# A two-layer diffusion backbone on one core: the opening of the second ConvFFN, the places of the last adaLN gate's additions, two product sums' places in the first ConvFFN, and copies ahead of casts on ScalarE

## The chip, the core and the metric

The kernel runs on one core of one Trainium2 chip. The time is device microseconds of one launch; the figure of a kernel is the median of its runs. A profile is one further execution, with its own time. Five engines work in parallel, each through its own list of instructions in order: PE (matrix products), DVE and ACT (elementwise work), POOL, and SP, which here issues most transfers from HBM. An instruction that must wait holds up everything behind it in its engine's list.

## The reference

512 latent tokens of width 1024 pass two layers. Layer 0 mixes tokens by attention, layer 1 by a Fourier transform. Every layer ends with a gated ConvFFN, which is where this change lies:

```python
def conv_ffn(h, w_up, conv_w, conv_b, w_down):
    u = h @ w_up                                   # 1024 -> 2 x 2816
    up = jnp.pad(u, ((0, 0), (1, 1), (0, 0)))
    u = up[:, :-2] * conv_w[0] + up[:, 1:-1] * conv_w[1] + up[:, 2:] * conv_w[2] + conv_b
    gate, val = jnp.split(u, 2, axis=-1)
    return (jax.nn.silu(gate) * val) @ w_down      # 2816 -> 1024
...
        sh1, sc1, g1, sh2, sc2, g2 = adaln_params(c, mod_w[i], mod_b[i])   # silu(c) @ mod_w[i] + mod_b[i], in six
...
        h = modulate(rms_norm(x, norm_g[i, 2]), sh2, sc2)
        x = x + g2 * rms_norm(conv_ffn(h, ffn_w_up[i], ffn_conv_w[i], ffn_conv_b[i], ffn_w_down[i]), norm_g[i, 3])
```

Each of the six adaLN vectors of a layer is a vector times a 1024x1024 matrix. The kernel calls the matrix `mod_r`, and computes most of these products in the shadow of other work.

## The kernel before

**Precision.** Every float32 product is made of three reduced-precision matmuls of 128x128 weights against 256 tokens (lines 108, 109 and 110): high part times high part, low times high, high times low. A weight tile is loaded raw from HBM; ACT casts it to the high part `wh`, and DVE subtracts to get the low part `wl` (both on line 144). The activations of a stage lie ready in pairs: `hh` and `hl` are the FFN's input, `xh` and `xl` (or `xT`) the gated results.

**ConvFFN.** The 2816 inner channels are 22 units of 128 channels, numbered 0 to 21; each has a gate half and a value half (two up products of 1024 by 128), a convolution (one ACT instruction on line 1485, two DVE instructions on lines 1486 and 1488 for each half), a silu, a product and a split into high and low. Units are collected in groups (`GROUPS`); a finished group is multiplied by its part of `w_down` in eight down tiles of 128 output channels. In FFN 1 (layer 1) the down tiles are spread among the units of the next group by the table `DOWN`: so many after unit so and so. What a down tile gives is added to `yT` by DVE (line 1511).

**Seven-product units.** Units in the table `SEVEN` compute both halves with seven products of half size instead of eight (a Strassen-like scheme). `seven_weights` loads the unit's two weight blocks, forms sums of them on DVE (lines 1389, 1391 and 1392) and then splits four pieces: "1", "57", "63" and "24", in that order. `seven_products` issues the products in the order "1", "5", "6", "2", "3", "4", "7" into two PSUM tiles `x` and `y`. Between them ACT copies halves of these tiles away (lines 1422, 1424 and 1426), since the next product but one overwrites or adds to them. After "3", DVE adds `xs` to `x` (line 1429); after "7" it adds `ys` to `y` (line 1433). "5" and "7" need the weights "57"; "6" and "3" need "63"; "2" and "4" need "24".

**The adaLN products** come in two forms. In FFN 0, `gemv_jobs` runs several of them one after the other, a step at a time, whenever the FFN calls `pump(gem, ...)`: each step is two DVE additions of a 128x1024 tile (line 594 or 597) and the next load of `mod_r`. At the end of one product `gemv_end` issues its "sums": four matmuls (line 639) that add up over partitions, an ACT copy, and later two transposes (line 649) and the vector's own small arithmetic on DVE. In FFN 1 `gemv_pair` does the last vector, the gate `g2` of layer 1: four pairs of additions (lines 627 and 629), each pair on two tiles `xh` and `xl` of 512 KB that one SP transfer each brings. These steps are pumped after the down tiles that `GEMV` names, group by group.

**Opening of FFN 1.** Units 0 to 2 begin while the normalisation before them is still being finished. `NSKEW[1]` is 5, so that five half-units are begun in the sweep; the sixth entry of `first` is unit 2's value half, and unit 3 (`FIRST`) is the first ordinary one. In the program `halves` are tokens 0 to 255 and 256 to 511, `hl` of the second half becomes ready piece by piece.

**What sets the order.** Nothing is written down as a fixed list: a scheduler orders each engine's instructions from the program's order, its dependences, `follow(a, b)` (a directly behind b), `behind_pe` (behind the PE work issued so far) and `held`. So a moved call can move other engines' rows too.

Of the kernel before, what the change touches and what calls it, by code (L numbers as in the profile page):

```python
# [2 lines left out]

# [7 lines left out]
F32 = mybir.dt.float32  # L11
# [4 lines left out]
ALU = mybir.AluOpType  # L16
# [3 lines left out]
P = 128  # L20
D = 1024
KC = D // P
T = 512
TT = T // P
HT = T // 2
# [7 lines left out]
FIRST = 3  # L33

SUMS = [5, 7]
# [1 line left out]
SEVEN = [(5, 6, 8, 10, 12, 14, 15, 17, 18, 20), (8, 9, 10, 11, 12, 13, 14, 15, 16, 17, 18, 19, 20, 21)]  # L37


GEMV = {0: (0, 5, 7), 1: (0, 2, 4, 6)}  # L40
DOWN = {8: 4, 9: 4, 10: 1, 11: 1, 12: 1, 13: 2, 14: 1, 15: 2, 16: 1, 17: 1, 18: 1, 19: 2, 20: 1, 21: 2}
NSKEW = [6, 5]
EPS = 1e-6
# [42 lines left out]
def kernel(ctx: ExitStack, tc: tile.TileContext, a):  # L86
    nc = tc.nc
# [55 lines left out]
    def split(h, l, src, eng=V):  # L143
        i = S.copy(out=h, in_=src), eng.tensor_tensor(out=l, in0=src, in1=f(h), op=ALU.subtract)  # L144
        for j in i:
            held(j)
        return i
# [414 lines left out]
    def gemv_jobs(jobs, pps, away=None):  # L562
        places = away and [xT[:, 4 * i:4 * i + 4, :].rearrange("p a b -> p (a b)").rearrange(
            "p (i d) -> p i d", i=2) for i in range(2)]
        todo = [(l, v, kk) for l, v in jobs for kk in range(4)]
        ws = []

        def load():
            if len(ws) < len(todo):
                l, v, kk = todo[len(ws)]  # L570
                src = a["mod_r"][6 * l + v - 2, kk]
                if not places:
                    ws.append(raw([P, 2, D], src))
                    return
                ws.append(places[len(ws) % 2])
                SY.dma_start(out=ws[-1], in_=src)

        if places:
            SY.dma_start(out=away, in_=xT)
            for _ in places:  # L580
                load()
            yield
        n = 0
        for l, v in jobs:
            acc = mk(cp, [P, D], F32, "gacc", 1)
            for kk in range(4):
                if not places:
                    load()
                w = ws[n]
                n += 1  # L590
                for i in range(2):
                    k = 2 * kk + i
                    if k == 0:
                        held(V.tensor_scalar(out=acc, in0=w[:, i, :], scalar1=scol[:, 0, k:k + 1], scalar2=None,
                                             op0=ALU.mult))
                    else:
                        held(V.scalar_tensor_tensor(out=acc, in0=w[:, i, :], scalar=scol[:, 0, k:k + 1], in1=acc,  # L597
                                                    op0=ALU.mult, op1=ALU.add))
                if places:
                    load()  # L600
                yield
            if places and (l, v) == jobs[-1]:
                SY.dma_start(out=xT, in_=away)
            end = gemv_end(l, v, acc, pps)
            next(end)
            yield
            if (l, v) == jobs[-1]:
                yield
            next(end, None)
# [3 lines left out]
    def gemv_pair(l, v, pps, xp):  # L613
        w = [mk(xp.first, [P, D], F32, n, 4) for n in ("xh", "xl")]

        def load(kk):
            for i in range(2):
                SY.dma_start(out=w[i], in_=a["mod_r"][6 * l + v - 2, kk][:, i, :])

        load(0)  # L620
        yield
        acc = mk(cp, [P, D], F32, "gacc", 1)
        for kk in range(4):
            for i in range(2):
                k = 2 * kk + i
                if k == 0:
                    V.tensor_scalar(out=acc, in0=w[i], scalar1=scol[:, 0, k:k + 1], scalar2=None, op0=ALU.mult)
                else:
                    V.scalar_tensor_tensor(out=acc, in0=w[i], scalar=scol[:, 0, k:k + 1], in1=acc, op0=ALU.mult,
                                           op1=ALU.add)  # L630
            if kk < 3:
                load(kk + 1)
            yield
        yield from gemv_end(l, v, acc, pps)
# [701 lines left out]
    def up_weights(l, pairs, fis, eng=V):  # L1336
        for fi in fis:
            r = raw([P, 2, KC, P], a["w_up"][l, fi])
            for i in range(2):
                wh, wl = pairs([P, KC, P])  # L1340
                split(wh, wl, r[:, i, :, :], eng)
                yield [(wh[:, k, :], wl[:, k, :]) for k in range(KC)]
# [27 lines left out]
    def seven_inputs(xp):  # L1370
# [10 lines left out]
            split(*b[n], src)  # L1381
        return b

    def seven_weights(l, fi):
        r = raw([P, 2, KC, P], a["w_up"][l, fi])
        s = mk(wp, [P, 4, KH, P], F32, "raw", 3)
        a4 = r.rearrange("p i (c k) n -> p (i c) k n", c=2)

        for j in (V.tensor_tensor(out=s[:, 0:2], in0=a4[:, 3::-3], in1=a4[:, 2].unsqueeze(1).to_broadcast(
                      [P, 2, KH, P]), op=ALU.add),  # L1390
                  V.tensor_tensor(out=s[:, 2], in0=s[:, 0], in1=a4[:, 0], op=ALU.add),
                  V.tensor_tensor(out=s[:, 3], in0=s[:, 2], in1=a4[:, 1], op=ALU.add)):
            held(j)
        w = {}
        for names, src in (("1", a4[:, 0:1]), ("57", s[:, 0:2]), ("63", s[:, 2:4]), ("24", a4[:, 1::2])):
            wh, wl = wpair([P, len(names), KH, P])
            split(wh, wl, src)
            for i, n in enumerate(names):
                w[n] = wh[:, i], wl[:, i]
        return w  # L1400


    def seven_products(l, fi, pps, bs):
        w = seven_weights(l, fi)
        x, y = (mk(pps, [P, T], F32, "mm", 6) for _ in range(2))
        xs, ys = (mk(cp, [P, T], F32, "sq", 2) for _ in range(2))
        begun, last = {}, []

        def product(n, ps, h):
            (wh, wl), (bh, bl) = w[n], bs[n]  # L1410
            new = id(ps) not in begun
            m = []
            for k in range(KH):
                m += mm3(ps[:, halves[h]], wh[:, k, :], wl[:, k, :], bh[:, k, :], bl[:, k, :], new and k == 0,
                         k == KH - 1, True)
            begun[id(ps)] = True
            if last:
                follow(m[0], last.pop())
            last.append(m[-1])

        product("1", y, 1)
        S.copy(out=xs[:, :HT], in_=y[:, HT:])  # L1422
        product("5", x, 1)
        S.copy(out=ys[:, HT:], in_=x[:, HT:])  # L1424
        product("6", y, 1)
        S.copy(out=xs[:, HT:], in_=y[:, HT:])
        product("2", x, 0)
        product("3", x, 1)
        V.tensor_tensor(out=x, in0=x, in1=xs, op=ALU.add)  # L1429
        product("4", y, 0)  # L1430
        product("7", y, 1)
        S.copy(out=ys[:, :HT], in_=y[:, HT:])
        V.tensor_tensor(out=y, in0=y, in1=ys, op=ALU.add)
        return x, y
# [27 lines left out]
    def ffn(l, xp, ready, pre, mid, gem, plain=None):  # L1462
# [5 lines left out]
        def up_mm(ps, w, sl, k0=0):  # L1468
            return [mm3(ps[:, sl], wh, wl, bh[:, sl], bl[:, sl], k == 0, k == KC - 1)
                    for k, ((wh, wl), (bh, bl)) in enumerate(zip(w, H)) if k >= k0]  # L1470
# [155 lines left out]
        cg = None  # L1626
        for u, (fi, i, w, ps) in enumerate(first):
            if u == skew:
                for s in halves:
                    up_mm(ps, w, s)  # L1630
            elif plain is None and u > 1:
                up_mm(ps, w, halves[1], 1)
            c = conv(fi, i, ps, (R, *(ub[:, n, i, fi:fi + 1] for n in (3, 1, 2))) if u < skew and plain else None)
            if i == 0:
                cg = c
            else:
                gated(fi, cg, c, 0)
# [5 lines left out]
        for gi, (f0, nch) in enumerate(GROUPS[l]):  # L1643
            end = gi == len(GROUPS[l]) - 1
            for fi in range(max(f0, FIRST), f0 + nch):
                if fi == SUMS[l]:
                    bs = seven_inputs(xp)
                if fi in SEVEN[l]:
                    cc = [conv(fi, i, u, None, i == 1) for i, u in enumerate(seven_products(l, fi, pps, bs))]
                else:  # L1650
                    cc = []
                    for i, w in enumerate(up_weights(l, wpair, [fi])):
                        ps = mk(pps, [P, T], F32, "mm", 6)
                        m = [up_mm(ps, w, s) for s in halves]
                        follow(m[1][0][0], m[0][-1][1])
                        cc.append(conv(fi, i, ps))
                gated(fi, cc[0], cc[1], f0)
                if l == 0 and fi not in SEVEN[l] and fi > FIRST + 4:
                    pump(gem, GP[0])
                if l:  # L1660
                    pump(down, DOWN.get(fi, 0))
# [88 lines left out]
    with ExitStack() as es:  # L1750
# [177 lines left out]
        xp = Pairs(ctx)  # L1928
# [180 lines left out]
```

## Time and profile before

| | |
|---|---|
| median of 3 runs | 1092.1 us (1091.9, 1092.1, 1093.35) |
| profiled execution, its own time | 1095.22 us |
| its span (what the trace covers) | 1093.5 us |
| PE, DVE, ACT busy | 1074.4, 887.3, 601.7 us |
| granted TensorE clock, mean | 0.999 |

Times in the trace count from the start of the span. FFN 0 runs from about 320 to 642 us, the Fourier mixer lies between, FFN 1 runs from about 745 to 1082 us, and a tail of 11 us ends the program. A row of the timeline gives start and duration in us, the engine, the line, the operation, output and inputs, a count, and in brackets how long the engine was idle before and what ended that. Matmul durations overlap: a 128x256 matmul shows about 0.28 us, but the next starts 0.11 to 0.12 us later, so a pause on PE is read from starts. DVE's rows overlap too, by 0.08 us.

### The profile page before, as it was taken

Reading aid. Unit: us, or ns where it says so; the run is one execution under the profiler, and the core shown is the slowest. Engines: PE = TensorE matmul, PEld = TensorE weight load, DVE = VectorE, ACT = ScalarE, POOL = GpSimd, SP = SyncE. Lnnn points to the kernel's source line nnn. Section 1 sums busy time; section 2 is a strip of 40 time slices with the busy share of each in tenths; the row PEclk is TensorE's granted clock in tenths of the full one; section 3 lists DMA queues with packets and bytes.
Section 4 is the critical chain, followed back from the end, with each engine's and each line's share of the span. In section 5 each row is a group of like instructions: output and inputs, shape, how many; then the busy total and the mean of one; then the engine's idle time right before and its main releaser. Section 6 shows DMA issues by size and latency. Waiting matters only on the chain.

```text
span 1093.5 us, 22646 instructions
## 1 busy us (share of the span) xinstructions
PE 1074.4 (98%) x9432; PEld 1012.8 (93%) x9432; DVE 887.3 (81%) x1454; ACT 601.7 (55%) x1053; POOL 104.6 (10%) x114
## 2 busy tenths in 40 slices
PE   9999999999999999999999999999999999999997
PEld 5699888869999999999999999989999999999996
DVE  5778877774679976877999877878997899889855
ACT  4442365675656633552465566767755465556533
POOL 0046122522100000000000020100000000000012
PEclk9999999999999999999999999999999999999999
DMA  9776101174231473426724620743205533323342
GB/s 364 287 260 212 40 1 40 43 271 188 78 155 40 154 251 143 186 88 229 263 83 153 229 107 2 237 149 120 99 26 162 205 106 112 117 82 108 111 150 78
DMA packets 33912, 156.55 MB, mean 143 GB/s; under 512 B 3472, under 2 KB 8208, under 8 KB 22160
## 3 DMA queue, kind: packets, MB, share of 16 engines
q1 hardware_dynamic: 32656, 150.89, 38.0%
q0 software_dynamic: 1152, 4.19, 1.6%
q8 instruction: 74, 1.21, 0.4%
q14 instruction: 30, 0.25, 0.1%
HBM read 148.78 MB, written 6.29 MB: 142 GB/s over the span
## 4 chain that ended last, share of the span: by engine, by line
PE 81%; DVE 9%; DMA 4%; ACT 3%; issue 2%; SPq 0%; POOL 0%; DVEq 0%; ACTq 0%; POOLq 0%
PE mm L108 23%; PE mm L109 22%; PE mm L110 22%; DVE wl L144 2%; PE PT L1147 1%; DMA raw<-in_w_up 1%; DVE gacc L597 1%; DMA xT<-in_xT 1%; PE gm L108 1%; PE O L109 1%; PE gm L109 1%; PE gm L110 1%; PE misc L211 1%; PE O L108 1%; PE O L110 1%
## 5 line engine op out<-in xcount | busy, mean ns | idle before, releaser
L144 ACT CAST wh<-raw 128x1024 fp32r<-128x1024 f32 (+2 forms) x206 | 190.2, 931 | 153.1 <-PE mm L109 101.6
L144 DVE TENSOR_TENSOR wl<-raw,wh 128x1024 fp32r<-128x1024 f32 (+2 forms) x206 | 220.1, 1074 | 25.6 <-ACT wh L144 25.4
L108 PE MATMUL mm<-hh,wh 128*128 128x256 f32 x852 | 237.7, 280 | 2.2 <-ACT sq L1424 1.1
L109 PE MATMUL mm<-hl,wh 128*128 128x256 f32 x852 | 236.9, 278 | 0.3 <-DVE hl L393 0.3
L110 PE MATMUL mm<-hh,wl 128*128 128x256 f32 x852 | 236.4, 278 | 0.7 <-DVE wl L144 0.7
L108 PEld LDWEIGHTS mm<-hh,wh 128*128 128x128 f32 x852 | 159.7, 188 | 4.5 <-ACT sq L1424 1.5
L110 PEld LDWEIGHTS mm<-hh,wl 128*128 128x128 f32 x852 | 160.8, 189 | 1.5 <-DVE wl L144 1.4
L109 PEld LDWEIGHTS mm<-hl,wh 128*128 128x128 f32 x852 | 160.0, 188 | 0.7 <-DVE hl L393 0.5
L108 PE MATMUL mm<-xh,wh 128*128 128x256 f32 x492 | 136.8, 279 | 0.0
L109 PE MATMUL mm<-xl,wh 128*128 128x256 f32 x492 | 136.5, 278 | 0.0
L110 PE MATMUL mm<-xh,wl 128*128 128x256 f32 x492 | 136.1, 277 | 0.0
L108 PE MATMUL mm<-zh,wh 128*128 128x256 f32 x384 | 106.8, 278 | 0.1
L109 PE MATMUL mm<-zl,wh 128*128 128x256 f32 x384 | 106.3, 277 | 0.0
L110 PE MATMUL mm<-zh,wl 128*128 128x256 f32 x384 | 106.3, 277 | 0.0
L108 PEld LDWEIGHTS mm<-xh,wh 128*128 128x128 f32 x492 | 92.4, 188 | 1.3 <-issue 0.4
L109 PEld LDWEIGHTS mm<-xl,wh 128*128 128x128 f32 x492 | 92.4, 188 | 0.5 <-issue 0.4
L110 PEld LDWEIGHTS mm<-xh,wl 128*128 128x128 f32 x492 | 92.4, 188 | 0.0
L318 POOL TENSOR_TENSOR cv<-cv,sq 128x256 f32<-128x256 f32 x20 | 16.6, 830 | 711.8 <-ACT sq L316 711.1
L108 PEld LDWEIGHTS mm<-zh,wh 128*128 128x128 f32 x384 | 72.1, 188 | 0.8 <-ACT sq L1422 0.3
L110 PEld LDWEIGHTS mm<-zh,wl 128*128 128x128 f32 x384 | 72.3, 188 | 0.0
L109 PEld LDWEIGHTS mm<-zl,wh 128*128 128x128 f32 x384 | 72.1, 188 | 0.0
L1485 ACT ACTIVATE cv<-mm,cols 128x512 f32<-128x512 f32 x59 | 45.7, 776 | 13.7 <-DVE mm L1429 6.5
(469 smaller groups left out, 2784.1 us busy)
## 6 DMA issues: line engine op xcount, KB each, us to landing
raw<-in_w_up SPq DMA_DIRECT2D x42, 1024.0 KB, 4.8
xT<-in_mod_r SPq DMA_DIRECT2D x20, 1024.0 KB, 5.0
raw<-in_w_down SPq DMA_DIRECT2D x32, 384.0 KB, 3.1
raw<-in_mod_p SPq DMA_DIRECT2D x8, 1024.0 KB, 4.8
raw<-in_w_down SPq DMA_DIRECT2D x16, 512.0 KB, 4.7
raw<-in_w_in SPq DMA_DIRECT2D x6, 1024.0 KB, 8.3
yT<-in_mod_r SPq DMA_DIRECT2D x10, 512.0 KB, 5.8
raw<-in_w_out SPq DMA_DIRECT2D x4, 1024.0 KB, 5.9
```

The costliest lines, as they stand in the source:

```text
L108: i = PE.matmul(out, lhsT=ah, rhs=bh, start=start, stop=False, skip_group_check=skip)
L109: PE.matmul(out, lhsT=ah, rhs=bl, start=False, stop=False, skip_group_check=skip)
L110: return i, PE.matmul(out, lhsT=al, rhs=bh, start=False, stop=stop, skip_group_check=skip)
L144: i = S.copy(out=h, in_=src), eng.tensor_tensor(out=l, in0=src, in1=f(h), op=ALU.subtract)
L211: PE.matmul(ps[32 * j:32 * j + 32, :w], lhsT=ones32, rhs=sq[:, j * w:(j + 1) * w], start=first, stop=last)
L318: G.tensor_tensor(out=self.acc[:, sl], in0=self.acc[:, sl], in1=sq[:, sl], op=ALU.add)
L597: held(V.scalar_tensor_tensor(out=acc, in0=w[:, i, :], scalar=scol[:, 0, k:k + 1], in1=acc, op0=ALU.mult, op1=ALU.add))
L1147: PE.transpose(out=pt[:, j * P:(j + 1) * P], in_=Ps[j][:, off:off + P], identity=ident)
L1485: S.activation(out=cv, in_=ps, func=AF.Identity, bias=bc, scale=wc[1])
```

## The change

Five things, in the order of the program:

1. In FFN 0's `gemv_jobs`, for the third and the fourth product (jobs 2 and 3, `GAP = 2`): the third's sums are issued one pump later, its successor's first step runs without a pause behind that, and the fourth's sums are put behind the PE work issued so far.
2. In FFN 1 the sixth entry of the opening and unit 3's gate half (`FIRST`) are issued by halves of tokens: first half of the one, first half of the other, then the second halves.
3. `seven_inputs` of FFN 1 is called after unit 7 instead of before it.
4. `gemv_pair`'s additions are pumped at other places (`GEMV`), and each is given a dependence without a semaphore on the DVE instruction issued just before its pair, so that the scheduler can't move it ahead of that.
5. The copy after "6" of one seven-product unit is followed by the next unit's first cast on ACT.

```diff
-GEMV = {0: (0, 5, 7), 1: (0, 2, 4, 6)}
+GEMV = {0: (0, 7), 1: (1, 3, 5), 2: (0, 2)}
+GAP = 2
...
-                yield
+                if not (places and job == GAP + 1 and kk == 0):
+                    yield
...
             end = gemv_end(l, v, acc, pps)
-            next(end)
+            if places and job == GAP:
+                yield
+            if places and job == GAP + 1:
+                behind_pe(end)
+            else:
+                next(end)
...
         for kk in range(4):
+            last = [o for o in nc.cur_bb.bb.instructions if o.engine == mybir.EngineType.DVE][-1].name
             for i in range(2):
...
+                tc.add_manual_dep(j.ins, last, mybir.DependencyInfo(
+                    mybir.DependencyClass.NoSync, mybir.DependencyReason.DATA), reason="order")
...
-            split(wh, wl, src)
+            c = split(wh, wl, src)[0]
+            if names == "1" and copied:
+                follow(c, copied.pop())
...
-        S.copy(out=xs[:, HT:], in_=y[:, HT:])
+        copied.append(S.copy(out=xs[:, HT:], in_=y[:, HT:]))
...
             if u == skew:
-                for s in halves:
-                    up_mm(ps, w, s)
+                m = [up_mm(ps, w, halves[0])]
+                ahead = up_weights(l, wpair, [FIRST])
+                wa = next(ahead)
+                pa = mk(pps, [P, T], F32, "mm", 6)
+                m += [up_mm(pa, wa, halves[0]), up_mm(ps, w, halves[1])]
+                for j in (1, 2):
+                    follow(m[j][0][0], m[j - 1][-1][1])
...
-                if fi == SUMS[l]:
+                if fi == SUMS[l] and fi in SEVEN[l]:
                     bs = seven_inputs(xp)
...
+                    if fi == SUMS[l]:
+                        bs = seven_inputs(xp)
```

In the changed program the lines above carry other numbers: 108 to 110 become 110 to 112, 144 becomes 146, 1389, 1391 and 1392 become 1402, 1404 and 1405, 1422, 1424 and 1426 become 1437, 1439 and 1441, 1429 and 1433 become 1444 and 1448, 627 and 629 become 636 and 638, 1485, 1486 and 1488 become 1500, 1501 and 1503, 1511 becomes 1526. No engine's count of instructions changes. The rows below give a place in an engine's list, the line, the operation, output and inputs; the numbers behind a tile's name tell its copies apart.

**First place: PE at the opening of FFN 1.** `mm_9394` is the sixth entry of the opening. Before, after 24 matmuls on its first half of tokens:

```order
L110 MATMUL mm_9394<-hh_69,wl_9086 128x256
L108 MATMUL mm_9394<-hh_69,wh_9085 128x256
L109 MATMUL mm_9394<-hl_71,wh_9085 128x256
L110 MATMUL mm_9394<-hh_69,wl_9086 128x256
L108 MATMUL mm_9394<-hh_69,wh_9085 128x256
```

and now, with `mm_9478` the gate half of unit 3:

```order
L112 MATMUL mm_9394<-hh_69,wl_9086 128x256
L110 MATMUL mm_9478<-hh_69,wh_9474 128x256
L111 MATMUL mm_9478<-hl_71,wh_9474 128x256
L112 MATMUL mm_9478<-hh_69,wl_9475 128x256
L110 MATMUL mm_9478<-hh_69,wh_9474 128x256
```

Between the two halves of the sixth entry stand now 24 matmuls of unit 3 on the first half.

**Second place: ACT between units 11 and 12 of FFN 1.** The three copies of unit 11 are those into `sq`; the cast of 128x512 is the first of unit 12. Before:

```order
L1422 COPY sq_10681<-mm_10680 128x256
L144 CAST wh_10839<-raw_10833 128x512
L1424 COPY sq_10682<-mm_10679 128x256
L1426 COPY sq_10681<-mm_10680 128x256
L144 CAST wh_10843<-raw_10835 128x1024
```

and now:

```order
L1437 COPY sq_10677<-mm_10676 128x256
L1439 COPY sq_10678<-mm_10675 128x256
L1441 COPY sq_10677<-mm_10676 128x256
L146 CAST wh_10831<-raw_10825 128x512
L146 CAST wh_10835<-raw_10827 128x1024
```

The cast, which waits for a load, stood ahead of two copies that only wait for PE; now it stands behind them.

**Third place: DVE at unit 15 of FFN 1.** `mm_11423` (before) and `mm_11415` (now) are unit 14's tile `x`; the raw tile is that of unit 15's weight sums. The beginning of the block before:

```order
L1389 TENSOR_TENSOR raw_11577<-raw_11575 128x1024
L1511 TENSOR_TENSOR yT_68<-yT_68,mm_11357 128x512
L144 TENSOR_TENSOR wl_11534<-raw_11531,wh_11533 128x768
L1391 TENSOR_TENSOR raw_11577<-raw_11577,raw_11575 128x512
L144 TENSOR_TENSOR wl_11582<-raw_11575,wh_11581 128x512
L1392 TENSOR_TENSOR raw_11577<-raw_11577,raw_11575 128x512
L1429 TENSOR_TENSOR mm_11423<-mm_11423,sq_11425 128x512
```

and now, all of its rows that the prediction counts (in two pieces):

```order
L1444 TENSOR_TENSOR mm_11415<-mm_11415,sq_11417 128x512
L1402 TENSOR_TENSOR raw_11571<-raw_11569 128x1024
L146 TENSOR_TENSOR wl_11576<-raw_11569,wh_11575 128x512
L1501 SCALAR_TENSOR_TENSOR cv_1416_11509<-mm_11415,cols_64,cv_1416_11509 128x511
L1404 TENSOR_TENSOR raw_11571<-raw_11571,raw_11569 128x512
L1448 TENSOR_TENSOR mm_11416<-mm_11416,sq_11418 128x512
L1503 SCALAR_TENSOR_TENSOR cv_1416_11509<-mm_11415,cols_64,cv_1416_11509 128x511
L1405 TENSOR_TENSOR raw_11571<-raw_11571,raw_11569 128x512
```

```order
L1501 SCALAR_TENSOR_TENSOR cv_1417_11513<-mm_11416,ncw_9535,cv_1417_11513 128x511
L146 TENSOR_TENSOR wl_11580<-raw_11571,wh_11579 128x1024
L1503 SCALAR_TENSOR_TENSOR cv_1417_11513<-mm_11416,ncw_9535,cv_1417_11513 128x511
L1526 TENSOR_TENSOR yT_68<-yT_68,mm_11529 128x512
L1514 TENSOR_TENSOR cv_1417_11513<-cv_1416_11509,cv_1417_11513 128x512
L638 SCALAR_TENSOR_TENSOR gacc_10648<-xh_10292,cols_64,gacc_10648 128x1024
L146 TENSOR_TENSOR wl_11584<-raw_11571,wh_11583 128x1024
L638 SCALAR_TENSOR_TENSOR gacc_10648<-xl_10293,cols_64,gacc_10648 128x1024
L146 TENSOR_TENSOR wl_11588<-raw_11569,wh_11587 128x1024
```

Unit 14's addition into `x` stands now ahead of unit 15's weight sums, and the fourth pair of the gate's additions stands ahead of and behind the low part of "63" (`wl_11584`), ahead of that of "24" (`wl_11588`). On PE the four sums of the gate, which stood ahead of unit 14's product "1", now stand behind the second matmul of unit 15's "2".

More of the change, by code (lines that the diff above doesn't have):

```diff
@@ L1 @@
 import math
+from itertools import chain
 from contextlib import ExitStack, contextmanager
@@ L583, in gemv_jobs @@
         n = 0
-        for l, v in jobs:
+        for job, (l, v) in enumerate(jobs):
             acc = mk(cp, [P, D], F32, "gacc", 1)
@@ L626, in gemv_pair @@
                 if k == 0:
-                    V.tensor_scalar(out=acc, in0=w[i], scalar1=scol[:, 0, k:k + 1], scalar2=None, op0=ALU.mult)
+                    j = V.tensor_scalar(out=acc, in0=w[i], scalar1=scol[:, 0, k:k + 1], scalar2=None, op0=ALU.mult)
                 else:
-                    V.scalar_tensor_tensor(out=acc, in0=w[i], scalar=scol[:, 0, k:k + 1], in1=acc, op0=ALU.mult,
-                                           op1=ALU.add)
+                    j = V.scalar_tensor_tensor(out=acc, in0=w[i], scalar=scol[:, 0, k:k + 1], in1=acc, op0=ALU.mult,
+                                               op1=ALU.add)
+                tc.add_manual_dep(j.ins, last, mybir.DependencyInfo(
+                    mybir.DependencyClass.NoSync, mybir.DependencyReason.DATA), reason="order")
             if kk < 3:
@@ L1382, in seven_inputs @@
         return b
+    copied = []
     def seven_weights(l, fi):
@@ L1651, in ffn @@
                     cc = []
[L1652 to L1655, printed above, removed]
+                    given = l and fi == FIRST
+                    for i, w in enumerate(chain([wa], ahead) if given else up_weights(l, wpair, [fi])):
+                        if given and i == 0:
+                            ps = pa
+                            up_mm(ps, w, halves[1])
+                        else:
+                            ps = mk(pps, [P, T], F32, "mm", 6)
+                            m = [up_mm(ps, w, s) for s in halves]
+                            follow(m[1][0][0], m[0][-1][1])
                         cc.append(conv(fi, i, ps))
+                    if fi == SUMS[l]:
+                        bs = seven_inputs(xp)
                 gated(fi, cc[0], cc[1], f0)
```

## The prediction

> **What bounds the kernel now.** I read the busy shares on the page first, then the two FFN stretches by windows, then who PE waited for there, and last the timelines around each of those waits.
>
> ```profile
> PE 1074.4 (98%) x9432; PEld 1012.8 (93%) x9432; DVE 887.3 (81%) x1454; ACT 601.7 (55%) x1053; POOL 104.6 (10%) x114
> ```
> ```profile
> 440.00:642.00 202.00, 199.91 (x1756) 196.68 (x1756) 177.82 (x230) 105.21 (x164) 5.34 (x6) 1.00 0.47 170
> 746.00:1068.00 322.00, 320.52 (x2805) 318.78 (x2805) 281.10 (x389) 188.35 (x296) 4.88 (x6) 1.00 0.33 113
> ```
>
> In the windows the columns are the length, then busy time and count of PE, weight loads, DVE, ACT and POOL, then the granted clock. PE is the bound, and in the part of the FFNs that the change touches it idles 2.1 us of 202 and 1.5 of 322. No count changes, so there is only this idle time to be won, and nothing to stop new idle time from being lost. Whom PE waited for, first between 440 and 650 us, then between 740 and 1080:
>
> ```profile
> PE misc L639 <- DVE gacc L597: 0.8, 1, 0.8
> PE mm L110 <- DVE wl L144: 0.7, 2, 0.4
> PE mm L108 <- ACT wh L144: 0.5, 1, 0.5
> ...
> PE mm L108 <- ACT sq L1424: 1.1, 1, 1.1
> PE mm L109 <- DVE hl L393: 0.3, 1, 0.3
> ```
>
> These are all of PE's waits in the two stretches. A second thing shows in windows of 30 us each, two from a slow stretch and two from fast ones:
>
> ```profile
> 780.00:810.00 30.00, 30.00 (x257) 30.00 (x256) 29.92 (x41) 16.77 (x24) 0.00 (x0) 1.00 0.10 36
> 820.00:850.00 30.00, 30.00 (x257) 30.00 (x257) 22.92 (x30) 16.01 (x28) 0.00 (x0) 1.00 0.53 167
> 440.00:470.00 30.00, 30.00 (x267) 30.00 (x267) 26.51 (x34) 17.63 (x27) 0.00 (x0) 1.00 0.39 147
> 890.00:920.00 30.00, 30.00 (x267) 30.00 (x267) 29.14 (x38) 18.81 (x30) 0.00 (x0) 1.00 0.33 111
> ```
>
> PE is fully busy in all four at a clock of 1.00, yet runs 257 matmuls in two of them and 267 in the others. With 0.28 us of overlap at the edges that is one per 117.8 ns or one per 113.4. The DMA share (0.10 and 0.53 against 0.39 and 0.33) doesn't separate them. I come back to it among the rivals.
>
> **The change part by part.**
>
> *FFN 0, third sums.*
>
> ```profile
> 512.66 1.28 DVE L597 SCALAR_TENSOR_TENSOR gacc<-xT,cols,gacc 128x1024 f32<-128x1024 f32 x1
> 513.86 0.95 DVE L144 TENSOR_TENSOR wl<-raw,wh 128x768 fp32r<-128x768 f32 x1
> ...
> 512.87 0.28 PE L108 MATMUL mm<-xh,wh 128*128 128x256 f32 x1
> 513.99 0.64 PE L639 MATMUL misc<-gacc,ones 128*32 128x256 f32 x8 [0.84 <-DVE gacc L597]
> ```
>
> The sums started 1.12 us behind the matmul ahead of them, against 0.11 ordinarily, since the last addition ended at 513.94. They now stand one down tile (36 matmuls, 36 x 0.113 = 4.1 us) later, long after that. PE gains 1.0 us here.
>
> *FFN 0, fourth sums.* They stood inside unit 15, between the first matmuls of unit 16 and product "6":
>
> ```profile
> 538.50 1.22 DVE L144 TENSOR_TENSOR wl<-raw,wh 128x1024 fp32r<-128x1024 f32 x1
> 539.63 0.70 DVE L1429 TENSOR_TENSOR mm<-mm,sq 128x512 f32<-128x512 f32 x1
> ...
> 544.30 0.39 PE L108 MATMUL mm<-hh,wh 128*128 128x256 f32 x1 [0.52 <-ACT wh L144]
> 544.73 0.64 PE L639 MATMUL misc<-gacc,ones 128*32 128x256 f32 x8
> 545.78 0.39 PE L110 MATMUL mm<-hh,wl 128*128 128x256 f32 x1 [0.42 <-DVE wl L144]
> 546.01 0.28 PE L108 MATMUL mm<-zh,wh 128*128 128x256 f32 x1
> ```
>
> Now the sums and the L110 that waited for DVE stand behind unit 16. The addition at 539.63 stands ahead of the low part at 538.50, so what ACT does behind it, up to the cast that ended the wait at 544.30, can come 1.13 us earlier. "6" would start at 543.4 instead of 546.01; less 0.68 us for the sums and the L110, which only move, that is 1.9 us, the first term's 1.0 included, because PE comes to this wait earlier and waits longer. Against it: the fourth product's additions start about one addition (1.20 us, the step from 512.66 to 513.86) later in a list that is solid here. I take 1.9 - 1.2 = 0.7 us for both terms together; the ends are a gain of 1.9 and a loss of 0.5, if two additions get in the way.
>
> *FFN 1, opening.*
>
> ```profile
> 753.13 1.22 DVE L144 TENSOR_TENSOR wl<-raw,wh 128x1024 fp32r<-128x1024 f32 x1
> 762.41 0.69 DVE L393 TENSOR_TENSOR hl<-yT,hh 128x512 fp32r<-128x512 f32 x1
> ...
> 762.54 0.28 PE L108 MATMUL mm<-hh,wh 128*128 128x256 f32 x1
> 763.16 0.39 PE L109 MATMUL mm<-hl,wh 128*128 128x256 f32 x1 [0.34 <-DVE hl L393]
> ```
>
> A low part of the input's second half that PE wants at 762.65 is there at 763.10. The start at 763.16 is 0.5 us late, and a further 0.15 us is lost around it; the table of waits shows no other wait for the input, so the first half was there in time. Between the halves stand now 24 matmuls (2.7 us) of unit 3 on that first half, with weights of which DVE made the low part from 753.13 on, so the second half is asked for 2.7 us later. Gain 0.65 us; the ends are 0.3 (the later low parts become late instead) and 0.7. The move of `seven_inputs` behind unit 7 lets unit 7's two low parts go first; PE waited for neither, and I cost it at nothing under the cover of unit 7's own 96 matmuls.
>
> *FFN 1, copies ahead of casts.*
>
> ```profile
> 882.87 0.62 ACT L144 CAST wh<-raw 128x512 fp32r<-128x512 f32 x1 [1.83 <-DMA raw<-in_w_up]
> 883.39 0.37 ACT L1424 COPY sq<-mm 128x256 f32<-128x256 f32 x1
> ...
> 868.46 0.28 PE L110 MATMUL mm<-zh,wl 128*128 128x256 f32 x1
> 868.82 0.39 PE L108 MATMUL mm<-hh,wh 128*128 128x256 f32 x1
> 882.47 0.28 PE L110 MATMUL mm<-zh,wl 128*128 128x256 f32 x1
> 883.81 0.38 PE L108 MATMUL mm<-hh,wh 128*128 128x256 f32 x1 [1.06 <-ACT sq L1424]
> ```
>
> At 882.87 the cast waited for a load that was queued behind the gate's loads; the copy behind it, which needed only PE, came at 883.39, and PE's "2" started 1.34 us behind the matmul ahead, so 1.22 too late. One unit earlier the cast and the copy stand in the same order, and there 0.36 lies between 868.46 and 868.82, where the slow rate would have 0.12: 0.24 too late. With the copies first both go: 1.46 us. Behind the copies the cast is hardly later than the load lets it be, and its user, the next unit's "1", is 72 matmuls and a down tile away, some 10 us.
>
> *FFN 1, the gate's additions.* They leave a stretch where they waited for loads and come to units 10, 12, 14 and 15. In 10 and 12 DVE has slack. In the block of unit 15 it has not. The durations there, from the same block before:
>
> ```profile
> 932.57 0.70 DVE L1429 TENSOR_TENSOR mm<-mm,sq 128x512 f32<-128x512 f32 x1 [2.92 <-PE mm L110]
> ...
> 935.27 1.22 DVE L144 TENSOR_TENSOR wl<-raw,wh 128x1024 fp32r<-128x1024 f32 x1
> 936.40 0.75 DVE L1488 SCALAR_TENSOR_TENSOR cv<-mm,cols,cv 128x511 f32<-128x511 f32 x1
> 937.06 0.69 DVE L1433 TENSOR_TENSOR mm<-mm,sq 128x512 f32<-128x512 f32 x1
> 937.66 1.22 DVE L144 TENSOR_TENSOR wl<-raw,wh 128x1024 fp32r<-128x1024 f32 x1
> ...
> 932.30 0.28 PE L108 MATMUL mm<-zh,wh 128*128 128x256 f32 x1
> ```
>
> The steps are 1.13 us for 1024 elements, 0.66 for a convolution instruction, 0.60 for 512 elements, and 1.20 for a gate's addition. Unit 14's addition into `x` waited for "3" (its last matmul is the one before 932.30) while the weight sums of unit 15 were already done. Now it stands ahead of them. From it up to the end of the low part of "63" the new list has seven steps of 0.60, four of 0.66, three of 1.13, one addition of 1.20, and 0.1 for the end: 4.2 + 2.64 + 3.39 + 1.2 + 0.1 = 11.5. So "63" is ready at 944.1. PE from 932.30 has 24 matmuls, a down tile's 36, "1" and "5" with 24, and two of "6" until it needs it: 86 x 0.1133 = 9.74, so at 942.0. The wait is 2.1; I take 2.0. "24" comes after one more addition, 2.3 us behind "63", against 12 matmuls and the sums, 1.9 us: 0.4 more. Unit 14 by the same count (13.9 us of DVE that begin 0.27 behind "3", against 124 matmuls, 14.05) loses 0.1 to 0.2, and unit 19, where the addition into `x` again goes first, one step of 0.6. Together a loss of 3.2 us less what DVE catches up while PE stands, which I don't count; the ends are 1.5 and 5. The sums of the gate only move.
>
> *Sum.* -0.7 - 0.65 - 1.46 + 3.2 = +0.4 us, within ends of about -2 and +3.5. Against the profiled execution's 1095.22 us that gives 1095.6; the median of the runs shown is 3.1 us below that execution, and carried over the forecast is 1092.1 + 0.4 = 1092.5 us.
>
> **The rivals.**
>
> *Faster, by the matmul's rate.* In the profile the slow rate begins behind the stop at 763 to 766 and ends with the stop at 868. Over those 102 us there were some 866 matmuls; at 113.3 ns instead of 117.8 they would take 3.9 us less. The change takes away both stops, and ahead of the first one the rate was fast. If it stays so, the time is 1092.5 - 3.9 = 1088.6. For it: the rates change only at such stops. Against it: the timed runs were already 3.1 us under this execution and may have run fast there. The Trainium skill, "TensorE: Matmul & The Clock Gate", section "Back-to-back issue gap", gives an isolated gap of N/2.4 + 2.5 ns, so 109 ns for 256 columns, one figure for a shape, and says that in a stream the spacing is set by weight load and matmul together. By its formula there is no second rate and this rival is empty; this trace, with 257 and 267 in windows of equal clock, differs, and the measurement decides.
>
> *Slower, by the same.* The new wait at unit 15 is a stop too. If the slow rate begins there and lasts to 1068, some 123 us or 1050 matmuls cost 4.5 ns each: +4.7, and the time is 1097.2. Against it: the stops at 514, 544, 868 and 883 were all followed by the fast rate.
>
> *Slower, by a late load.*
>
> ```profile
> 920.18 0.33 SPq L154 DMA_DIRECT2D raw<-in_w_up  x1
> 925.15 1.23 DVE L1389 TENSOR_TENSOR raw<-raw 128x1024 f32<-128x1024 f32 x1 [0.65 <-DMA raw<-in_w_up]
> ```
>
> In SP's new list unit 15's weights stand behind the gate's last pair of loads, and these wait for the third pair of additions, in unit 14's block, so until about 926.4 instead of 920.2. The weight sums want it at 933.2. A load took 4.8 us before (issued 920.18, sums released 925.15), and with 512 KB of the gate's own ahead of it perhaps 6.5, so it comes about when wanted. Each us beyond is a us of PE. If it lands after 935 the time is over 1094.3; I put this case at 1095.0.
>
> *Faster, by slack that I miss.* DVE may do unit 15's block in time, if rows of it find their inputs earlier than the list suggests; then the gains of 2.8 us stand alone, 1092.1 - 2.8 = 1089.3. Against it: every step counted is an instruction that can't be left out. I count it with the first rival.
>
> **How the numbers follow.** My forecast (1092.5) has 0.42, the fast rate or no loss at unit 15 0.34, the slow rate 0.10, the late load 0.14. A measurement of this kernel can tell about 0.2%, 2.2 us, from no change: its three runs span 1.45 us. Faster by that takes 0.30 from the second case and 0.04 from the first, 0.34; slower takes 0.08, 0.10 and 0.04, 0.22; 0.44 remains. The range of 8 in 10 reaches from 1087.8, the fast rate with a little more, to 1095.8, which leaves out most of the slow rate and the worst late loads. The likeliest case alone has 1090.5 to 1094.5.
>
> **What would show it.** Right: no pause of PE ahead of the third sums in FFN 0 and none near 763; copies of lines 1437 to 1441 without a cast between them; a pause of about 2 us of PE in unit 15's "6" that ends with a low part on line 146; 257 or 267 matmuls in 30 us, as before. Wrong: no pause at unit 15 (then DVE had slack that I don't see), a wait of the weight sums for `in_w_up` there, or 267 between 770 and 868.

## The result and the profile after

The changed kernel is slower: 1104.1 us in the median of six runs (1099.5 to 1108.6) against 1093.5 us of the kernel before in the same session, a ratio of 1.0098 with a 95% interval of 1.0069 to 1.0128. A second session gave 1.0103 (1.0083 to 1.0122). The forecast was 1092.5 us, and the range ended at 1095.8.

The trace shown below is of an execution of 1099.48 us (span 1097.7). Its windows, with the columns of those shown of before (the windows of 30 us are three of the same four):

```profile
440.00:642.00 202.00, 200.36 (x1772) 196.98 (x1771) 177.74 (x232) 105.61 (x167) 5.34 (x6) 1.00 0.47 169
746.00:1068.00 322.00, 315.17 (x2717) 312.50 (x2716) 277.20 (x378) 184.93 (x290) 4.15 (x5) 1.00 0.32 109
780.00:810.00 30.00, 30.00 (x266) 29.96 (x265) 30.00 (x37) 15.78 (x22) 0.00 (x0) 1.00 0.14 45
820.00:850.00 30.00, 30.00 (x255) 30.00 (x256) 20.90 (x29) 15.69 (x28) 0.00 (x0) 1.00 0.43 148
440.00:470.00 30.00, 30.00 (x268) 30.00 (x266) 27.27 (x35) 17.57 (x27) 0.00 (x0) 1.00 0.33 120
```

FFN 0 is as it was, and in FFN 1 PE idles 6.8 us where it idled 1.5. Whom PE waited for between 440 and 650 us, and then between 740 and 1076:

```profile
PE mm L110 <- ACT sq L1437: 1.0, 1, 1.0
PE mm L112 <- DVE wl L146: 0.5, 1, 0.5
...
PE mm L112 <- DVE wl L146: 4.7, 4, 2.2
PE mm L110 <- ACT sq L1437: 1.9, 2, 1.4
```

Of the waits of before one is left, for a low part in FFN 0: it lasted 0.3 us at 576.57 and lasts 0.5 us at 573.26 now. The others are gone, and others have come. The largest ones are at unit 15, on PE:

```profile
935.57 0.28 PE L111 MATMUL mm<-zl,wh 128*128 128x256 f32 x1
937.87 0.39 PE L112 MATMUL mm<-zh,wl 128*128 128x256 f32 x1 [2.03 <-DVE wl L146]
...
939.56 0.28 PE L111 MATMUL mm<-xl,wh 128*128 128x256 f32 x1
942.06 0.39 PE L112 MATMUL mm<-zh,wl 128*128 128x256 f32 x1 [2.21 <-DVE wl L146]
```

Product "5" stood still for 2.2 us for the low part of "57", and "6" for 2.4 us for that of "63". What DVE did there, and SP's issues ahead of it:

```profile
927.79 0.70 DVE L1444 TENSOR_TENSOR mm<-mm,sq 128x512 f32<-128x512 f32 x1 [2.30 <-PE mm L112]
931.08 1.23 DVE L1402 TENSOR_TENSOR raw<-raw 128x1024 f32<-128x1024 f32 x1 [2.59 <-DMA raw<-in_w_up]
...
936.60 1.22 DVE L146 TENSOR_TENSOR wl<-raw,wh 128x1024 fp32r<-128x1024 f32 x1
...
939.59 1.28 DVE L638 SCALAR_TENSOR_TENSOR gacc<-xh,cols,gacc 128x1024 f32<-128x1024 f32 x1
940.78 1.22 DVE L146 TENSOR_TENSOR wl<-raw,wh 128x1024 fp32r<-128x1024 f32 x1
```
```profile
919.98 0.33 SPq L626 DMA_DIRECT2D xh<-in_mod_r  x1
921.77 0.33 SPq L626 DMA_DIRECT2D xl<-in_mod_r  x1
923.54 0.33 SPq L156 DMA_DIRECT2D raw<-in_w_up  x1
```

DVE waited 2.3 us for PE at unit 14's addition into `x`, then 2.6 us for unit 15's weights, which came 7.5 us after their issue, and from then on worked without a gap, with the gate's addition at 939.59 ahead of the low part that PE was waiting for.

**An account by pauses and rate.** A matmul of 256 tokens starts 113.3 ns behind the one ahead at the fast rate. I took from each trace two sums over PE's starts: the pauses (all that a step beyond 135 ns has over 113.3), and the slow rate's excess (what steps from 106 to 135 ns have over 113.3). The time of the profiled execution less both sums is 971.9 to 972.3 us in 15 of the 16 traces of this study, and 972.8 in the other. So a time here is 972.1 us plus pauses plus excess. Most of this is bookkeeping, since every kernel has the same 9432 matmuls; what it adds is that nothing else in a trace differs by more than 1 us. In the table the pauses are split by stage (of FFN 1, the part up to 885 us and that of units 12 to 20).

In four traces a part of the last stage's pauses lies in a stretch of 3.4 us in which the clock granted to PE is half. It begins at the end of the stops of unit 15, and a matmul in it starts 0.21 us behind the one ahead. First the third trace of the changed kernel, then the first one in the same window (columns: window, length, busy time and count of PE, clock, DMA):

```profile
942.10:945.50 3.40, 3.40 (x20) 0.50 0.59 199
```
```profile
942.10:945.50 3.40, 3.32 (x29) 1.00 0.46 135
```

This is 2.0 us of the 10.0 in that row of the table, 2.0 of the 9.3 without the two pairs' transfers, 1.7 of the 8.2 of the gate alone, and 1.6 of the 7.9 without the fourth pair's additions.

| kernel | profiled us | pauses FFN 0 | FFN 1 to 885 | 885 to 1060 | excess, all | ratio of the runs to before (95%) |
|---|---|---|---|---|---|---|
| before | 1095.2 | 7.2 | 3.5 | 0.6 | 12.9 | 1 |
| changed | 1099.5 | 7.6 | 2.5 | 8.6 | 9.1 | 1.0098 (1.0069, 1.0128) |
| changed, second trace | 1100.3 | 7.4 | 0.7 | 8.4 | 12.0 | 1.0103 (1.0083, 1.0122) |
| changed, third | 1099.4 | 7.2 | 2.5 | 10.0 | 6.9 | one execution |
| changed, fourth | 1100.6 | 8.0 | 2.5 | 7.9 | 9.8 | one execution |
| gate put back | 1093.5 | 6.7 | 2.6 | 0.6 | 11.5 | 1.0003 (0.9991, 1.0016) |
| gate alone | 1104.9 | 5.4 | 2.7 | 8.2 | 17.5 | 1.0102 (1.0077, 1.0128) |
| opening alone | 1094.3 | 6.7 | 1.9 | 0.6 | 13.3 | 1.0016 (1.0006, 1.0027) |
| copies and FFN 0 alone | 1092.9 | 8.0 | 2.3 | 0.6 | 10.6 | 1.0011 (0.9996, 1.0026) |
| tie at the old places | 1090.5 | 6.7 | 2.6 | 2.3 | 7.1 | 1.0008 (0.9993, 1.0022) |
| new places, no tie | 1095.8 | 7.3 | 3.9 | 0.9 | 11.1 | 1.0026 (1.0008, 1.0045) |
| two pairs' transfers left out | 1098.1 | 7.3 | 2.5 | 9.3 | 7.1 | 1.0075 (1.0058, 1.0093) |
| fourth pair's additions left out | 1103.0 | 6.7 | 0.7 | 7.9 | 15.4 | 1.0106 (1.0072, 1.0139) |
| third and fourth left out | 1100.6 | 7.8 | 3.4 | 2.1 | 15.7 | 1.0033 (1.0013, 1.0053) |
| order of the change without its additions | 1095.6 | 6.7 | 0.7 | 3.4 | 13.0 | 1.0027 (1.0008, 1.0046) |
| its additions without its order | 1098.1 | 7.6 | 1.2 | 1.7 | 14.9 | 1.0031 (1.0016, 1.0046) |

The four traces of the changed kernel agree in one thing: 7.9 to 10.0 us of pauses from unit 12 on (7.9 to 8.6 without the half clock), against 0.6.

### The profile page after: what moved, and what is told of

Its sections match the earlier page's. It is cut to its first block, busy times and chain, and to the rows that moved or that the text cites. A ratio compares the mean times of both kernels' runs of the same rounds, so it can differ in the third digit from the quotient of the medians.

```text
span 1097.7 us, 22650 instructions
## 1 busy us (share of the span) xinstructions
PE 1072.9 (98%) x9432; PEld 1009.8 (92%) x9432; DVE 886.3 (81%) x1454; ACT 600.0 (55%) x1053; POOL 104.5 (10%) x114
```

## The experiments

**Which part of the change, and the changed kernel a second time.** `after_again`, `after_t3` and `after_t4` are the changed kernel itself. `gate_back` is the changed kernel with this undone; `gate_only` is the kernel before with only this done:

```diff
-GEMV = {0: (0, 5, 7), 1: (0, 2, 4, 6)}
+GEMV = {0: (0, 7), 1: (1, 3, 5), 2: (0, 2)}
...
+                tc.add_manual_dep(j.ins, last, ...)   # for each of the gate's additions
```

`open_only` is the kernel before with only FFN 1's opening and the later `seven_inputs`.

> The changed kernel once more, for a second trace. Its first profiled execution took 1099.5 us, while its other timed runs took 1103.6 to 1108.6. If the gate's additions are the cause (theory G), the pauses of PE at units 15 to 20 are there again, 6.5 us or more of them, and longer by the late load of unit 15's weights. If the matmul's rate is the cause of the rest (theory R), the pauses are the same as in the first trace within 1 us and a stretch of 100 us or more has 257 matmuls in 30 us where the first trace had 267. If the load times vary (theory D), the pause ahead of unit 15's 6 differs by more than 1 us from the first trace's 2.2 and 2.4.

> The changed kernel with the gate's additions at their old places and without their added dependence. Theory G: no pauses at units 13 to 20 beyond 0.3 us each, and 1089 to 1093 us, no slower than before. Theory O (the opening makes the loss): still the pause of 1.6 us near 820 us and a time of 1098 or more. Theory R: the time depends on the stops left, 1088 to 1098.

> The kernel before with only the gate's additions moved and tied. Theory G: nearly the whole loss, 1100 to 1106 us, with pauses at units 14 to 20 of 6 us or more. Theory O: at most 3 us above before, 1093 to 1096.

> The kernel before with only the second FFN's opening changed and its seven_inputs call behind unit 7. Theory G: the stop at 763 is gone, 0.65 us, and the time is 1091 to 1094. Theory O: the pause near 820 (1.6 us in the changed kernel) shows here too, since DVE is the bound from 766 to 820 and PE only runs into it sooner; the time is 1093 to 1097.

The gate's new places, with their tie, carry the whole loss: alone they give 1.0102, and without them the rest of the change gives 1.0003. The second trace of the changed kernel has the pauses of the first within 0.2 us from unit 12 on, and the slow rate between 770 and 818 us, where the first has the fast one. The opening alone is not faster but 0.06 to 0.27% slower, though its stop near 763 is gone. Near 820 the changed kernel has a pause of 1.6 us that the kernel before has not. On ACT, and on PE behind it:

```profile
818.95 0.62 ACT L146 CAST wh<-raw 128x512 fp32r<-128x512 f32 x1 [0.58 <-DMA raw<-in_w_down]
819.47 0.36 ACT L1437 COPY sq<-mm 128x256 f32<-128x256 f32 x1
...
819.89 0.39 PE L110 MATMUL mm<-zh,wh 128*128 128x256 f32 x1 [1.43 <-ACT sq L1437]
```

It is the stop that the copies' tie was made against, with a down tile's cast in the place of the unit's first cast. `gate_back` has it too (1.6 us at 822), `after_again` and `open_only` have not. The difference is the rate of PE ahead of it. First `after_again`, whose windows run at the slow rate, then `gate_back`, whose windows run at the fast one (columns: window, length, busy time and count of PE, clock, DMA):

```profile
770.00:818.00 48.00, 48.00 (x410) 1.00 0.15 51
```
```profile
770.00:818.00 48.00, 48.00 (x425) 1.00 0.14 50
```

In the window from 780 to 810 DVE is busy for 29.92 and 30.00 of 30 us before and after. There DVE sets the pace, and a faster PE only meets its next wait sooner: 15 more matmuls in 48 us are 1.7 us won, and the pause is 1.6. The first two traces of the changed kernel show it on one program. The weight sums of line 1402 start at 807.32 in the first and 808.08 in the second, so DVE is 0.8 us apart; PE, at the fast rate in the first, is 2.6 us apart at 815, and behind the first trace's pause 1.2 us. Of the 1.9 us that the rate had won, 0.4 are left.

**Transfers, tie and places.** `no_loads34` is the changed kernel without the transfers for the last two pairs (`if kk < 1` for `if kk < 3`); `nodep` is without the added dependence; `tie_old_places` has the old `GEMV` with the dependence; `copies_gap` is the kernel before with only the copies' tie and FFN 0's sums.

> The changed kernel without the four transfers that bring the gate's tiles for the third and fourth pairs of additions; the additions stay and read the tiles of the second pair, so the gate comes out of part of its matrix. DVE's list is the same. Theory L (the late load of unit 15's weights starts it, and each later unit's load is then late in turn): the weight sums of unit 15 no longer wait for their load, the pauses ahead of unit 15's 6 shrink from 4.6 to about 2.0 us, those of units 16 to 20 go from 2.1 to under 0.8, and the time is 1096 to 1099. Theory A (the additions' place in DVE's list alone): pauses and time stay as in the changed kernel, 1102 to 1105.

> The changed kernel without the tie, so that the additions are called at the new places, but the scheduler sets them earlier in DVE's list, three pairs of them ahead of unit 12. Theories L and A both: nothing of the gate stands in the blocks of units 13 to 16, no pauses there, 1091 to 1095. If the new call places are at fault by something else (the places of sums and transposes on PE): 1098 or more.

> The changed kernel with the tie, but with the additions at the places of the kernel before (pairs in the blocks of units 10 or 11, 11, 12 or 13 and 13 or 14), the last pair one unit and a half ahead of where the change has it. Theory A: a pair of additions costs 2.4 us of a block whose slack on DVE is about 2.9, so it is hidden as long as the load is early: 1090 to 1094. Theory L: the loads of the gate again stand ahead of w_up loads; a late load shows at unit 12 or 14 and the time is 1095 or more.

> The kernel before with only the copies ahead of the casts and the later sums of the first FFN; the opening and the gate as before. If the four stops they remove (1.0 us near 514, 0.7 near 545, 0.24 and 1.22 near 868 and 884) are worth what they last: 1089.5 to 1091.5, 2 to 3 us under the kernel before. If PE only runs sooner into the next wait, or the matmul's rate changes: within 1 us of before.

Without the transfers unit 15's weights were issued at 923.48, as in the changed kernel, but the sums could begin at once:

```profile
927.71 0.70 DVE L1444 TENSOR_TENSOR mm<-mm,sq 128x512 f32<-128x512 f32 x1 [2.29 <-PE mm L112]
928.32 1.22 DVE L1402 TENSOR_TENSOR raw<-raw 128x1024 f32<-128x1024 f32 x1
```

So the gate's 1 MB in flight made that load 2.6 us late; it didn't hold back its issue, which waits for a buffer that DVE frees. By the ratios the runs are about 0.3% faster than the changed kernel's, with intervals that overlap. The pauses of this trace are hardly fewer, though (9.3 us, 7.3 without the half clock): unit 15 lost 2.1 us instead of 4.6 in its large stops, but at the fast rate, which this trace has up to there, unit 14 lost 1.8 us, and the units behind 15 lost 3.0 us, as in the changed kernel (3.1). Theory L as I had it falls: a late load isn't needed to start the later pauses. Untied, the additions stand mostly ahead of unit 12, and the pauses go (0.9). Tied at the old places, where the last pair stands ahead of unit 14's weight sums, they cost at most 0.2%. `copies_gap` removes three stops of before and is not measurably faster.

**Which additions, and more traces.** `no_adds34` and `no_adds4` leave out the additions of pairs 3 and 4, or of pair 4 (`range(2 if kk < 2 else 0)`, `range(2 if kk < 3 else 0)`).

> The changed kernel again, for a third trace. Its first two traces were taken in executions of 1099.5 and 1100.3 us, while the median of its runs is about 1104. If the slower executions have more of the slow matmul rate (theory R): this trace, when it is 1102 or more, has the same pauses between 885 and 1060 (8.4 to 8.6 us there) within 1 us, and more stretches with 257 matmuls in 30 us. If they have later loads (theory D): the pauses themselves are 10 us or more.

> The same for a fourth trace, with the same numbers for each theory.

> The changed kernel without the gate's third and fourth pairs of additions (4.8 us of DVE); all transfers stay. The gate comes out of half its matrix. The weight sums stand ahead of the addition into x again from unit 15 on. Theory A: no pause over 0.3 us at units 15 to 20, the time that of the version with the gate put back, 1091 to 1095. If the transfers alone are enough to delay unit 15's weights: a pause of 1 us or more stays there and 1096 or more.

> The changed kernel without the fourth pair of additions only; its transfers stay, and at unit 15 the addition into x still stands ahead of the weight sums. The gate comes out of three quarters of its matrix. If each addition costs what it lasts: the pauses at unit 15 shrink from 4.6 + 0.4 to about 3.4 us and the time falls by 1.5 to 2, to 1101 to 1103. If the order and the late load carry the cost, the pauses of units 16 to 20 stay at about 2 us; if the backlog does, they vanish and the time is 1098 to 1100.

Without pair 4 the runs win nothing that they could show: 1.0106, from 1.0072 to 1.0139. The trace has less waiting, though. At unit 15 it has one stop of 2.1 us, at product "1", instead of 2.2 and 2.4, and of its 7.9 us of pauses 1.6 are the half clock; the units behind lose 3.0 us as before. So in this one trace pair 4 is worth about 2 us of pauses at unit 15, near its own 2.4, and the trace's 15.4 us of slow rate hide them in the time. Without both pairs 2.1 us are left. What changes between the two besides the additions is DVE's order: with pair 3 left out, too, the weight sums of units 15, 16, 19 and 20 stand ahead of the addition into `x` again. The third and fourth traces have the pauses of the first two and no more of the slow rate; both executions stayed under the 1102 us at which the expectation would have told the theories apart.

**Order against additions.** `sums_first` is the changed kernel with this, `x_first` is `gate_back` with the opposite tie:

```diff
         for j in (... the three weight sums ...):
             held(j)
+        if l and added and 14 <= fi <= 20:
+            for o in added[-2:]:                      # the additions into x and y of the unit before
+                tc.add_manual_dep(o.ins, j.ins.name, ...)
```
```diff
             held(j)
+            if l and added and fi in (14, 15, 16, 19, 20):
+                follow(j, added[-1])                  # the addition into x of the unit before
```

> The changed kernel with one more tie: at units 14 to 20 the weight sums of a unit stand ahead of the additions into x and y of the unit before. The gate's additions stay in the blocks of units 14 and 15, but at unit 15 now behind all of its low parts, and unit 15's load stands ahead of the gate's last loads. Order theory: no pause over 0.5 us at units 15 to 20 and 1091 to 1095. Additions theory (4.8 us of DVE in two blocks can't be hidden): pauses of 3 us or more remain and 1098 or more.

> The version with the gate put back, with the opposite tie: at units 14, 15, 16, 19 and 20 the addition into x stands ahead of the next unit's weight sums, as the scheduler has it in the changed kernel, but without any of the gate's additions or transfers there. Order theory: pauses of PE at these units, 3 us or more in all, and 1096 to 1101. Additions theory: DVE has its slack of about 3 us a unit, no pause over 0.5 us, and 1091 to 1095.

Neither theory alone holds. The order alone gives 3.4 us of pauses (2.8 more than `gate_back`) and 1.0027; the additions in their new blocks, with the sums first, give 1.7 us and 1.0031. Together they give 8 to 10 us and 1.010. `sums_first` isn't a clean half, though: its fourth pair stands behind unit 15's low parts and not among them, and unit 15's load is issued ahead of the gate's last loads (920.56 against 925.59), so it takes away the backlog and the late load of unit 15 along with the order. What DVE waited for between 895 and 1010 us tells how they join. The changed kernel:

```profile
DVE raw L1402 <- DMA raw<-in_w_up: 6.3, 4, 2.6
DVE mm L1444 <- PE mm L112: 6.2, 4, 2.3
```

`gate_back`, `x_first` and `sums_first`, in this order:

```profile
DVE mm L1441 <- PE mm L112: 3.4, 5, 1.1
DVE raw L1399 <- DMA raw<-in_w_up: 1.3, 2, 0.7
```
```profile
DVE mm L1444 <- PE mm L112: 5.2, 5, 2.6
DVE raw L1400 <- DMA raw<-in_w_up: 3.9, 2, 2.6
```
```profile
DVE mm L1449 <- PE mm L112: 3.6, 4, 1.2
DVE raw L1403 <- DMA raw<-in_w_up: 2.5, 1, 2.5
```

The wait for PE alone is not the difference. The kernel before has it too:

```profile
DVE mm L1429 <- PE mm L110: 6.3, 5, 2.9
DVE raw L1389 <- DMA raw<-in_w_up: 1.1, 2, 0.6
```

There the next unit's sums are done when DVE waits. With the addition into `x` first, DVE waits with these sums still to do. Its work on that unit then ends late, and with it the buffer comes free late into which the next unit's weights go. A row of SP and one of DVE in the changed kernel, two units on, and what SP waited for between 900 and 995 us:

```profile
959.25 0.33 SPq L156 DMA_DIRECT2D raw<-in_w_up  x1
...
964.29 1.23 DVE L1402 TENSOR_TENSOR raw<-raw 128x1024 f32<-128x1024 f32 x1 [2.52 <-DMA raw<-in_w_up]
...
SPq L156 <- DVE wl L146: 77.2, 14, 16.1
```

The load is issued when DVE has freed the buffer, takes 5.0 us, and DVE waits for it: each unit hands its delay to the next through the buffer, without any of the gate's work in it. The additions lengthen the first of these rounds, and the order takes away the slack in which DVE would catch up. That the order alone isn't enough is shown by `x_first`. That the additions with the sums first aren't enough is shown by `sums_first` only together with its earlier load and later fourth pair. That the buffer is the link is read from the rows; no run with one more buffer was made.

No version tried is faster than the kernel before by more than its interval.

## Why the prediction was wrong, point by point

The sum was +0.4 us, and the runs lost 10.6. Two steps of it failed: the gains of 2.8 us, of which the runs show none, and the loss of 3.2 us at the gate's additions, which is 8.0 us of pauses in the trace. What the runs lost beyond that stays open.

- **FFN 0: right in the place, wrong in the worth.** The third sums stand 0.2 us behind the matmul ahead now, so their stop is gone. The gain forecast was 0.7 us. From 480 to 640 us, where it was to come, the pauses are 4.3 to 5.4 us in four traces, against 5.2; the two kernels without this part of the change have 3.3 (`gate_only`) and 4.6 (`open_only`) there, so no gain is shown. The step that failed is the start of unit 15's "6": I let it go when the cast is done. In its place came the copy of "1", which ACT does behind the cast and an activation:

```profile
538.97 1.05 ACT L146 CAST wh<-raw 128x1024 fp32r<-128x1024 f32 x1
540.45 0.77 ACT L1500 ACTIVATE cv<-mm,cols,ncw 128x512 f32<-128x512 f32 x1
541.11 0.37 ACT L1437 COPY sq<-mm 128x256 f32<-128x256 f32 x1
...
541.53 0.38 PE L110 MATMUL mm<-zh,wh 128*128 128x256 f32 x1 [0.96 <-ACT sq L1437]
```

- **Opening and copies: the stops went as forecast, the time did not.** No trace of the changed kernel has the stops of 763, 868 or 884. The 2.1 us forecast for them came out as 1.0 less of pauses up to 885 in three traces and 2.8 less in the one at the slow rate, because of the new pause near 820. Neither is a gain of the runs: `gate_back`, which has these parts, gives 1.0003. I had looked for the opening's cover at the place itself, and not at the next engine that sets the pace: the row for 780 to 810, with DVE busy for 29.92 of 30, stood in the prediction and was read for PE's count alone.

- **The gate: the mechanism right at unit 15, its size and its sequel wrong.** Forecast 2.0 + 0.4 us at unit 15; measured 2.2 + 2.4 + 0.35. The count of DVE's steps holds: from 927.79 to the end of the low part of "63" at 942.0 are 14.2 us, and without the 2.6 of the late load 11.6, where I had 11.5. The late load was a rival with a chance of 0.14, issued 6.8 us ahead of its use and landing in 6.5, "about when wanted". It was issued 4.9 us ahead (923.54 against 928.4) and took 7.5, behind two transfers of 512 KB and not one; the wait it left wasn't a rare case but there in all four traces (1.9 to 2.6 us), and the sum has no term for it. Unit 14's margin of 0.2 us is a matter of the rate: nothing lost at the slow rate, 1.0 us in the third trace of the changed kernel, 1.8 without the transfers. The units behind 15 were forecast at 0.6 and lost 3.1 us (947 to 1060 us). The step that failed there is the end of the sum: it lets one later unit pay one step, puts the others at nothing, and speaks of "what DVE catches up while PE stands". In these rows DVE doesn't catch up, since its next load hangs on its own lateness (6.3 us of waits for loads against 1.1 before). In all 3.2 us were forecast, and the trace has 8.0 us more than before.

- **The rate.** The rivals of the rate were the right thing to doubt a time by: the excess ranges from 6.9 to 17.5 us over the traces, as much as the whole loss. The fast-rate rival failed for the changed kernel, since it gained in one stretch and paid at 820. The Trainium skill, "TensorE: Matmul & The Clock Gate", section "Back-to-back issue gap", gives one isolated gap for a shape at the full clock; the 16 traces have two rates at a granted clock of 1.00, and both are longer than the 109 ns that its formula makes of 256 columns (an estimate). The prediction's "the rates change only at such stops" doesn't hold throughout: in the first trace of the changed kernel the slow rate ends near 924 us with no step over 124 ns.

- **What stays open.** The pauses and rates of the four traces explain executions of 1099 to 1101 us. The eight runs without a profile took 1102.2 to 1108.6, and no trace shows all of what they have more. The half clock may be a part: their mean granted clock is 0.996 to 0.999, at most 0.998 in six of the eight, against one of 23 runs of the kernel before in the second session. Half clock for 3.4 us costs some 1.7 us and lowers the mean by 0.0015 (an estimate from the trace that has it), so that 0.996 is 3 to 4 us, not 8; and a mean of 0.998 can also come from the last microseconds alone, as in `nodep`. `gate_only` and `no_adds4`, at 1104.9 and 1103.0, have the same pauses (8.2 and 7.9) and 17.5 and 15.4 us of slow rate, so that the slow rate would be enough; that it was so in the runs of the changed kernel isn't shown. Nor is it known what makes a stretch run at one rate or the other, or why the clock halved in four of the traces with a stop at unit 15 and not in the others.

## What to carry to other kernels

A tie that fixes one engine's work at a place fixes what stands behind it too: look in the new order not only at the moved instructions but at those that now wait for another engine ahead of work that was ready (here the weight sums behind an addition that waits for PE). Where a load can be issued only when the same engine frees its buffer, a delay isn't caught up but handed on, so price it for every round and not once. And before a stop is priced at what it lasts, look at who sets the pace in the next 50 us: where that is another engine, the time won is given back there.

## What the runs showed of the hardware that I had not expected

With one program the slow rate's excess differed between executions by 5 us (6.9 to 12.0 in four traces of the changed kernel), at a granted clock of 1.00 where it ran. It mostly began and ended at steps of 0.2 us or more. Behind the stops of unit 15 (2.1 us and more in all) the granted clock fell to 0.50 for 3.4 us in four traces and stayed at 1.00 in the first, second and fourth of the changed kernel, with stops of the same size. A 1 MB load took 7.5 us with 1 MB of other transfers issued in the 3.6 us before it, and under 4.9 us without them.
